# Gate tiles and dense tiles placed anew beside two recurrences, and an opening whose weights are issued ahead

## Chip, cores and metric

The program runs on one core of a Trainium2 chip. The metric is the device time of one execution in microseconds (us). TensorE (PE) is the matrix engine, PEld its weight loads, VectorE is DVE, ScalarE is ACT, GpSimd is POOL, and SyncE (SP) issues most DMAs.

## What is computed

Two layers of one trunk over 512 latent tokens (segment L) and 256 context tokens (segment C), 1024 channels wide. Each layer normalises its input, sends it through three mixers (RWKV-7, gated DeltaNet, attention), scales each branch by a gate computed from the same normalised input, and ends in a SwiGLU. In short:

```python
hx = modulate(rmsnorm(x, norm1[l]), sh1x, sc1x)
px = jnp.split(hx @ lp['w_in'], IN_SPLIT_POINTS, axis=-1)
ya_x, _ = rwkv_branch(hx, px[0], lp, st_a)
yb_x, _ = gdn_branch(hx, px[1], px[2], lp, st_b)
yc_x = attn_latent(px[3], px[4], kc, vc, lp, cos, sin)
gates = jax.nn.sigmoid(h @ lp['w_gate'] + lp['b_gate'])      # 3 x 1024 outputs
ga, gb, gc = jnp.split(gates, N_BRANCH, axis=-1)
m = ga * (ya @ lp['w_up_a']) + gb * (yb @ lp['w_up_b']) + gc * (yc @ lp['w_up_c'])
x = x + g1x * (m @ lp['w_out'])
x = x + g2x * swiglu(...)
```

The shifts, scales and gains (sh1x, sc1x and so on) are 6 x 1024 numbers per layer and token kind, made from the conditioning vectors by `ada_w`. In layer 0 both segments go through all of it; in the last layer the context is needed only for the states, keys and values.

## The kernel before

Channels lie on the 128 partitions, tokens along the free axis. A **dense tile** is one 128-column block of a weight matrix times the whole input: eight blocks of 128 channels, each as three fp32r products (`mm3`, lines 241 to 243: high part times high part, high times low, low times high). A tile with both segments is 24 matmuls of 512 columns (PSUM tile dL) and 24 of 256 (dC); a tile of L alone is the first 24. For each the weights are loaded by SP into `wst` (two buffers), cast by ACT to `whi` (line 227) and their rest taken by POOL as `wlo` (line 231). The 24 tiles of `w_gate` of a layer (`gate`, whose tanh on ACT is line 710) are needed only at the layer's end; their place is free.

A layer runs in this order: low-rank projections and DeltaNet's scalars (`lora_g`, `gdn_scalars`), attention, DeltaNet in two passes `p` of two heads, RWKV in four passes `j` of two heads, then the merge and the SwiGLU.

Both recurrences run over **groups** of four chunks. A pass has three: ("C", 0) the context, ("L", 0) and ("L", 1) the halves of the latent tokens. In a group some preparation (exponentials, small products, the inverse of a triangular matrix in `inverse`) precedes four **steps**, each of which needs the state that the step before left. A step's solve is line 1378 in DeltaNet and line 1074 in RWKV; stretches of a pass are given below from one solve to another. The dense tiles that fill the time beside a pass are a list `self.units`: in DeltaNet the six q, k, v tiles of the next pass (`g_tiles`), two z tiles and some gate tiles; in RWKV three r, k, v tiles of the next pass, its key norm (`r_knorm`) and some gate tiles. After a group is written, `fill(n)` writes the next n units. The tables `GD` and `RD` hold n, by pass and, in a pass, for the three groups. `flush` writes what is left, except two units in a DeltaNet pass, which stand one by one behind the two heads' output norms.

Instructions aren't run in the order written: a scheduler orders them on each engine from priorities and modelled costs, and the recurrences' groups are written under a raised priority (`HPG`, `HPR`), so that a unit written behind a group lands among its steps or among those of the groups before it.

The **opening** (`build`) loads the context, then four 512 KB tiles for the first ada block (`ada`: products of the conditioning vectors with a block of `ada_w` in `adaps`, a copy to `adasb`, and a transposing product in `adamp`), the latent tokens, the weights of the first low-rank projection, and three more ada blocks, with eight buffers for their tiles. Then `norm1` makes the normalised input `hh`, `hl`. The second low-rank projection's weights (256 to 383 of `l1`) are loaded and split inside `lora_g` in layer 0; in layer 1 they have been made ahead, as `self.second`.

Of the kernel before, what the change touches and what calls it, by code (L numbers as in the profile page):

```python
# [38 lines left out]
AD = (0, 1, 2, 3)  # L39
ORD = (1, 2, 3, 6, 5, 7, 4)  # L40
LOV = ((1,), (1, 3, 5))
GD = ((5, 4, 0), (5, 4, 0))
RD = ((4, 4, 0), (4, 4, 0), (4, 4, 0), (2, 2, 0))


PV = {}
# [157 lines left out]
class Prog:  # L204
# [75 lines left out]
    def build(self):  # L280
        nc, tc, A = self.nc, self.tc, self.A
        self.pend = {"L": [], "C": []}
        pool = lambda name, bufs=1, **k: tc.tile_pool(name=name, bufs=bufs, **k)
        with tc.block(name="whole", schedule_with_timeline_sim=True), pool("cst") as cst, pool("wp", 2) as wp, pool("pp", 2, space=bass.MemoryType.PSUM) as pp, \
                pool("dr", space=bass.MemoryType.DRAM) as dr, pool("hp") as hp, pool("sb", 2) as sb:
            self.cst, self.wp, self.pp, self.dr, self.hp, self.sb = cst, wp, pp, dr, hp, sb
            self.dC, self.dc = pp.tile([128, 2, TC], F32, name="dC", tag="dC", bufs=1), 0
            C = cst.tile([128, NCO], F32, name="C")
            nc.sync.dma_start(C, A["co"][:, 0:NCO])
            self.C = C  # L290
            self.scv = cst.tile([128, 8, 32], F32, name="scv")
            nc.sync.dma_start(self.scv, A["cv"])
            nc.scalar.activation(self.scv, self.scv, AF.Silu)
            self.xsrc = {"C": A["xT"][:, :, 0:TC], "L": A["xT"][:, :, TC:T]}
            self.vectors(0)
            with tc.tile_pool(name="nx", bufs=2, reuse_waits="tile") as nx:
                x = {}
                self.nb = 8
                self.segs = ["L", "C"]
                ss = self.sums()  # L300
                self.tables()
                for s, n in (("C", TC), ("L", TL)):
                    x[s] = nx.tile([128, KT, n], F32, name="x" + s, bufs=1)
                    nc.sync.dma_start(x[s], self.xsrc[s])
                    if s == "C":
                        self.ada(0, 0, nx, 8, bank=("dL", 2))
                    else:
                        self.first = self.split(self.lora(0, 384, 96, 2, nx)[:])
                    for k in range(KT):
                        self.squares(x[s][:, k, :], k, s, ss)  # L310
                    self.settle()
                    rs = sb.tile([128, TL + 4], F32, name="rs", tag="up", bufs=2)[:, :n]
                    self.rstd_from(rs, ss[s], 1.0 / D, self.co("cb", 0, 1))
                    for k in range(KT):
                        nc.vector.tensor_tensor(x[s][:, k, :], x[s][:, k, :], rs, ALU.mult)
                for i in range(1, 4):
                    self.ada(0, i, nx, 8, bank=("dL", 2))
                self.norm1(0, x, nx)
            for l in range(DEPTH):
                self.l, self.nb = l, SB[l]  # L320
                self.last = l == DEPTH - 1
                self.P, self.MOD = self.Ps[l], self.MODs[l]
                self.layer()
                if self.upto is not None and self.upto[0] == l:
                    break
# [9 lines left out]
        self.nc.sync.dma_start(self.Ps[l], self.A["pv"][l])  # L335
        self.MODs[l] = self.cst.tile([128, 48, 2], F32, name=f"MOD{l}")

    def ada(self, l, n, pool, bufs=4, share=False, tag="adaw", bank=("iv", 1)):

        nc, A = self.nc, self.A  # L340
        ps = self.pp.tile([128, 512], F32, name="adaps", tag=bank[0], bufs=bank[1])
# [7 lines left out]
                nc.tensor.matmul(ps[32 * g:32 * g + 32, :], self.scv[:, k, :], w[:, i, :], start=(k < 4), stop=(k >= 4))  # L349
        sb = pool.tile([128, 512], F32, name="adasb", tag="adasb", bufs=1)  # L350
        nc.scalar.copy(sb, ps)
        mp = self.pp.tile([128, 4, 2], F32, name="adamp", tag=bank[0], bufs=bank[1])
        for m in range(4):
            nc.tensor.matmul(mp[:, m, :], sb[:, 128 * m:128 * m + 128], self.co("sel2"), start=True, stop=True)
        ob, _ = PV["ada_b"]
# [237 lines left out]
    def layer(self):  # L593
# [14 lines left out]
        with pool("sx") as self.sx:  # L608
# [10 lines left out]
            with pool("sg") as self.sc:  # L619
# [4 lines left out]
                    u()  # L624
                for p in range(2):
                    self.units = (g_tiles(1) if p == 0 else []) + z_tiles(p)
                    if p == 1:
                        self.units += gates[:6]
                        del gates[:6]
                    self.settle()  # L630
                    self.g_begin(p)
                    for grp, n in zip((("C", 0), ("L", 0), ("L", 1)), GD[p]):
                        with tc.high_priority(offset=HPG[l]):
                            self.g_group(p, *grp)
                        self.fill(min(n, len(self.units) - 2))
                    self.flush(2)
                    for hh in range(2):
                        self.g_out(p, hh)
                        self.fill(1)
# [3 lines left out]
        with pool("sr") as self.sc:  # L643
# [16 lines left out]
            self.settle()  # L660
            for j in range(4):
                self.units = r_tiles(j + 1) if j < 3 else []
                take = len(gates) if j == 3 else 4
                self.units += gates[:take]
                del gates[:take]
                self.r_begin(j)
# [90 lines left out]
    def lora_g(self):  # L757

        nc, A, l, sc = self.nc, self.A, self.l, self.sc
        self.GC, self.BR, self.rw, self.re, gh = {}, {}, {}, {}, {}  # L760
        if l:
            wq, wm = self.second
        else:
            wq, wm = self.lora(l, 256, 128, 2, sc)
            wm = self.split(wm[:])
        ps = self.dense(*self.first, self.h, self.S12)
        for s in self.S12:
            n = TL if s == "L" else TC
# [965 lines left out]
```

## Time and profile before

| what | value |
|---|---|
| median of 3 runs | 3975.29 us (3964.88 to 3981.9) |
| the profiled execution | 3986.69 us, of which the span of its instructions is 3984.9 us |
| TensorE busy | 3572.3 us, 90% of the span |
| VectorE, ScalarE, GpSimd busy | 2426.7, 1681.5 and 1465.1 us |
| mean granted TensorE clock | 0.906 |
| read from and written to HBM | 257.87 and 34.23 MB |

The profile page counts an engine as busy while an instruction of it executes. PEclk is the share of full speed that TensorE's clock was granted: 1.00 is 2.4 GHz, 0.50 is 1.2 GHz. A row of the windows view gives a stretch's start and end in us from the span's start, its length, then for each engine the busy us and in brackets the instructions, then the mean granted clock, the share of the DMA engines' time, and GB/s. A row of the timeline gives start, length, engine, line, operation, tiles, shapes, and in square brackets how long the engine had been idle and what ended that.

### The profile page before, as it was taken

The numbers are of one execution on the slowest core, as the hardware profiler recorded it, in microseconds if no ns is written. First come the engines' busy times: TensorE is split into PE (matmuls) and PEld (weight loads), VectorE is DVE, ScalarE is ACT, GpSimd is POOL, SyncE is SP. The second block draws the span as 40 slices with busy tenths as digits, with TensorE's granted clock in tenths as the row PEclk, the third lists the DMA queues.
The fourth block names the chain that finished last, engine by engine and source line by source line (L and its number), as shares of the span: only waits on it lengthen the run. The fifth ranks groups of instructions, "written<-read, shape, count | busy, mean of one in ns | idle before, by whom it ended". The sixth has DMA issues, their size and how long they took to land. (4 is left out here: it accounts for less than half of the span.)

```text
span 3984.9 us, 69791 instructions
## 1 busy us (share of the span) xinstructions
PE 3572.3 (90%) x27704; PEld 2928.8 (73%) x27704; DVE 2426.7 (61%) x4776; ACT 1681.5 (42%) x3207; POOL 1465.1 (37%) x1738
## 2 busy tenths in 40 slices
PE   7987878999899989899999798889998999898998
PEld 4655667777777768789999656666777777677887
DVE  5386745326766746565555557965167786467776
ACT  5455534334444432333333646543343443234334
POOL 3223213244233315454444424414241333164554
PEclk7998878999799999999999899989796988699999
DMA  5501111111011126422222251102120111252232
GB/s 190 172 30 51 32 33 50 53 57 55 13 53 38 40 71 199 153 80 69 70 69 59 94 179 53 51 25 75 39 63 9 53 32 47 96 186 66 93 96 82
DMA packets 121174, 296.61 MB, mean 74 GB/s; under 512 B 15024, under 2 KB 41824, under 8 KB 120464
## 3 DMA queue, kind: packets, MB, share of 16 engines
q1 hardware_dynamic: 111408, 260.16, 20.9%
q0 software_dynamic: 9440, 31.99, 2.1%
q8 instruction: 218, 3.57, 0.4%
q14 instruction: 108, 0.88, 0.1%
HBM read 257.87 MB, written 34.23 MB: 73 GB/s over the span
## 5 line engine op out<-in xcount | busy, mean ns | idle before, releaser
L231 POOL TENSOR_TENSOR wlo<-wst,whi 128x512 fp32r<-128x512 f32 (+3 forms) x606 | 693.0, 1164 | 784.1 <-ACT whi L227 755.4
L227 ACT CAST whi<-wst 128x1024 fp32r<-128x1024 f32 (+3 forms) x303 | 266.0, 878 | 512.3 <-PE dC L243 193.4
L241 PE MATMUL dL<-hh,whi 128*128 128x512 f32 x1040 | 436.3, 420 | 21.3 <-ACT tg L710 4.5
L242 PE MATMUL dL<-hl,whi 128*128 128x512 f32 x1040 | 423.7, 407 | 3.7 <-DVE hl L407 2.3
L243 PE MATMUL dL<-hh,wlo 128*128 128x512 f32 x1040 | 422.8, 407 | 0.1
L241 PEld LDWEIGHTS dL<-hh,whi 128*128 128x128 f32 x1040 | 202.1, 194 | 79.6 <-issue 6.9
L242 PEld LDWEIGHTS dL<-hl,whi 128*128 128x128 f32 x1040 | 201.9, 194 | 51.5 <-issue 7.5
L241 PE MATMUL dC<-hh,whi 128*128 128x256 f32 x704 | 220.7, 313 | 18.4 <-ACT ct L371 9.3
L243 PEld LDWEIGHTS dL<-hh,wlo 128*128 128x128 f32 x1040 | 201.3, 194 | 48.3 <-issue 2.5
L242 PE MATMUL dC<-hl,whi 128*128 128x256 f32 x704 | 213.2, 303 | 4.8 <-DVE hl L407 2.4
L243 PE MATMUL dC<-hh,wlo 128*128 128x256 f32 x704 | 212.2, 301 | 0.0
L502 POOL TENSOR_TENSOR sl<-S,sh 128x512 fp32r<-128x512 f32 x110 | 152.7, 1392 | 154.8 <-ACT sh L501 115.4
L241 PE MATMUL q<-g2h,sh 128*128 128x384 f32 (+1 forms) x528 | 166.8, 318 | 16.3 <-DVE c L524 13.8
L241 PEld LDWEIGHTS dC<-hh,whi 128*128 128x128 f32 x704 | 144.9, 206 | 35.3 <-ACT ct L371 11.9
L242 PE MATMUL q<-g2l,sh 128*128 128x384 f32 (+1 forms) x528 | 166.6, 316 | 2.9 <-DVE g2l L447 2.9
L243 PE MATMUL q<-g2h,sl 128*128 128x384 f32 (+1 forms) x528 | 165.1, 314 | 0.0
L242 PEld LDWEIGHTS dC<-hl,whi 128*128 128x128 f32 x704 | 145.2, 206 | 13.0 <-issue 3.9
L501 ACT CAST sh<-S 128x512 fp32r<-128x512 f32 x176 | 105.0, 619 | 105.0 <-PE q L242 63.7
L243 PEld LDWEIGHTS dC<-hh,wlo 128*128 128x128 f32 x704 | 145.1, 206 | 3.2 <-issue 1.7
L524 DVE TENSOR_TENSOR c<-c,q 128x384 f32<-128x384 f32 (+1 forms) x220 | 106.0, 482 | 61.7 <-PE q L243 50.6
L241 PE MATMUL dL<-fh,whi 128*128 128x512 f32 x352 | 138.3, 393 | 3.0 <-ACT fh L578 1.6
L242 PE MATMUL dL<-fl,whi 128*128 128x512 f32 x352 | 138.1, 392 | 0.0
(545 smaller groups left out, 10008.8 us busy)
## 6 DMA issues: line engine op xcount, KB each, us to landing
adaw<-in_ada SPq DMA_DIRECT2D x96, 512.0 KB
wst<-in_win SPq DMA_DIRECT2D x68, 512.0 KB
wst<-in_wg SPq DMA_DIRECT2D x48, 512.0 KB
w<-in_f SPq DMA_DIRECT2D x45, 512.0 KB
wst<-in_f SPq DMA_DIRECT2D x43, 512.0 KB
t<-tg POOLq DMA_DIRECT2D x48, 256.0 KB, 2.6
tgL<-t SPq DMA_DIRECT2D x48, 256.0 KB
wst<-in_f SPq DMA_DIRECT2D x48, 256.0 KB
```

The lines of the kernel that those rows point to most:

```text
L227: nc.scalar.copy(hi, wt)
L231: nc.gpsimd.tensor_tensor(lo[:, a:b], wt[:, a:b], hi[:, a:b].bitcast(F32), ALU.subtract)
L241: nc.tensor.matmul(ps, wh, xh, start=first, stop=False)
L242: nc.tensor.matmul(ps, wh, xl, start=False, stop=False)
L243: nc.tensor.matmul(ps, wl, xh, start=False, stop=last)
L501: nc.scalar.copy(hi, src)
L502: (nc.vector if i in LOV[l] else nc.gpsimd).tensor_tensor(lo, src, hi[:].bitcast(F32), ALU.subtract)
L524: add = lambda d, a, b: nc.vector.tensor_tensor(d, a, b, ALU.add)
```

## The change

Four edits. The tables: of a layer's 24 gate tiles, four stand in DeltaNet's first pass and eight in its second (before, none and six); RWKV's first three passes have two each (before, four), its last the six that are left, as before. The numbers behind the groups are (4, 4, 2) in DeltaNet's first pass, (3, 3, 2) in its second, (2, 2, 2) in RWKV's first three and, as before, (2, 2, 0) in its last. In the opening, ada blocks 1 to 3 are written ahead of the first low-rank projection's weights, with 12 buffers in place of 8, and `adamp` takes another PSUM tag (`ch`) than `adaps`. And the second low-rank projection's weights are loaded and split ahead of `norm1`, in layer 0 as in layer 1. The matmuls are the same in number and shape.

```diff
-GD = ((5, 4, 0), (5, 4, 0))
-RD = ((4, 4, 0), (4, 4, 0), (4, 4, 0), (2, 2, 0))
+GD = ((4, 4, 2), (3, 3, 2))
+RD = ((2, 2, 2), (2, 2, 2), (2, 2, 2), (2, 2, 0))
...
-                        self.ada(0, 0, nx, 8, bank=("dL", 2))
+                        self.ada(0, 0, nx, 12, bank=("dL", 2), mbank=("ch", 2))
                     else:
+
+                        for i in range(1, 4):
+                            self.ada(0, i, nx, 12, bank=("dL", 2), mbank=("ch", 2))
                         self.first = self.split(self.lora(0, 384, 96, 2, nx)[:])
...
-                for i in range(1, 4):
-                    self.ada(0, i, nx, 8, bank=("dL", 2))
+                wq, wm = self.lora(0, 256, 128, 2)
+                self.second = wq, self.split(wm[:])
                 self.norm1(0, x, nx)
...
-        mp = self.pp.tile([128, 4, 2], F32, name="adamp", tag=bank[0], bufs=bank[1])
+        mbank = mbank or bank
+        mp = self.pp.tile([128, 4, 2], F32, name="adamp", tag=mbank[0], bufs=mbank[1])
...
-                    if p == 1:
-                        self.units += gates[:6]
-                        del gates[:6]
+                    take = 8 if p else 4
+                    self.units += gates[:take]
+                    del gates[:take]
...
-                take = len(gates) if j == 3 else 4
+                take = len(gates) if j == 3 else 2
...
-        if l:
-            wq, wm = self.second
-        else:
-            wq, wm = self.lora(l, 256, 128, 2, sc)
-            wm = self.split(wm[:])
+        wq, wm = self.second
```

Three places show how the change moves instructions. First SP, the DMA queue of the opening: `adaw` are the ada blocks' tiles, `xL` the latent tokens, `l1w` the low-rank weights (96 and 128 columns wide), `wst` the first dense weights. Before:

```order
L345 DMA adaw<-in_ada 128x1024 x4
L304 DMA xL<-in_xT 128x8x512
L729 DMA l1w<-in_l 128x8x96
L345 DMA adaw<-in_ada 128x1024 x4
L236 DMA wst<-in_win 128x1024 x2
L335 DMA P_15142<-in_pv 128x233
L345 DMA adaw<-in_ada 128x1024 x8
L729 DMA l1w<-in_l 128x8x128
```

And in the changed kernel:

```order
L348 DMA adaw<-in_ada 128x1024 x4
L304 DMA xL<-in_xT 128x8x512
L348 DMA adaw<-in_ada 128x1024 x8
L733 DMA l1w<-in_l 128x8x96
L733 DMA l1w<-in_l 128x8x128
L338 DMA P_15142<-in_pv 128x233
L348 DMA adaw<-in_ada 128x1024 x4
L236 DMA wst<-in_win 128x1024
```

Two ada blocks now follow the latent tokens at once, both low-rank loads stand ahead of the last block, and the dense weights behind it.

Second ACT, in DeltaNet's first pass of layer 0, between the second and the third solve of group ("L", 0): `GUs` is the copy of a solve, `GS` the state, `go` the output, W and Y belong to the next group's inverse. Before:

```order
L1380 COPY GUs<-GU 128x256
L917 ACTIVATE W<-X,C 128x16x16
L1405 COPY go<-GSO 128x2x64
L1369 ACTIVATE GS<-GS,egl 128x128 x2
L917 ACTIVATE W<-X,C 128x16x16
L1405 COPY go<-GSO 128x2x64
L1369 ACTIVATE GS<-GS,egl 128x128 x2
L941 COPY Y<-ips 128x512
L1380 COPY GUs<-GU 128x256
```

One step of the same group in the changed kernel:

```order
L1380 COPY GUs<-GU 128x256
L917 ACTIVATE W<-X,C 128x16x16
L1405 COPY go<-GSO 128x2x64
L1369 ACTIVATE GS<-GS,egl 128x128 x2
L1405 COPY go<-GSO 128x2x64
L1369 ACTIVATE GS<-GS,egl 128x128 x2
L941 COPY Y<-ips 128x512
L714 ACTIVATE tg<-dL,hb 128x512
L227 CAST whi<-wst 128x1024
L1380 COPY GUs<-GU 128x256
```

A gate tile's tanh and the next tile's cast have come in between two solves that had no dense tile between them.

Third ACT, in RWKV's first pass of layer 0, around the third and fourth solve: `UV` is the copy of a solve, S the state, `tg` the tanh of a gate tile. Before:

```order
L951 COPY TT<-ips 32x8x32
L227 CAST whi<-wst 128x1024
L710 ACTIVATE tg<-dC,hb 128x256
L1075 COPY UV<-Up 64x2x64
L710 ACTIVATE tg<-dL,hb 128x512
L1067 ACTIVATE S<-S,EL 128x64 x2
L227 CAST whi<-wst 128x1024
L710 ACTIVATE tg<-dC,hb 128x256
L1075 COPY UV<-Up 64x2x64
```

And in the changed kernel:

```order
L951 COPY TT<-ips 32x8x32
L1075 COPY UV<-Up 64x2x64
L1067 ACTIVATE S<-S,EL 128x64 x2
L1075 COPY UV<-Up 64x2x64
```

The gate tiles that stood among these steps are gone, and no other dense tile has taken their place.

## Rows read from the trace of the kernel before

**Rows 1.** The page: busy time by engine, and the clock in 40 slices.

```profile
PE 3572.3 (90%) x27704; PEld 2928.8 (73%) x27704; DVE 2426.7 (61%) x4776; ACT 1681.5 (42%) x3207; POOL 1465.1 (37%) x1738
...
PEclk7998878999799999999999899989796988699999
```

**Rows 2.** The chain that ended last: two dense matmuls (start, us, what).

```profile
3937.44 0.12 PE dC L241
...
3955.03 0.23 PE dL L241
```

**Rows 3.** Windows: layer 0's DeltaNet stage.

```profile
335.00:813.00 478.00, 394.62 (x3231) 320.69 (x3230) 265.99 (x536) 210.15 (x398) 131.24 (x204) 0.84 0.16 47
```

**Rows 4.** Timeline of PE in the opening.

```profile
40.90 3.21 PE L349 MATMUL adaps<-adaw,scv 128*32 128x512 f32 x16
44.88 1.05 PE L354 MATMUL adamp<-C,adasb 128*128 128x2 f32 x8 [0.77 <-ACT adasb L351]
47.03 0.58 PE L241 MATMUL dC<-hh,whi 128*128 128x256 f32 x1 [1.10 <-ACT hh L405]
...
64.55 0.39 PE L243 MATMUL dL<-hh,wlo 128*128 128x512 f32 x1
68.63 0.39 PE L1205 MATMUL tsp<-C,gcC 40*64 40x8 f32 x4 [3.70 <-DVE gcC L1176]
...
93.22 0.73 PE L241 MATMUL dL<-ghgL,g2h 128*128 128x512 f32 x2
```

**Rows 5.** Timeline of SP: the load of the second low-rank weights.

```profile
50.45 0.55 SPq L729 DMA_DIRECT2D l1w<-in_l  x1
```

**Rows 6.** A window of the opening, for the last two columns (DMA share, GB/s).

```profile
20.00:30.00 10.00, 5.23 (x14) 0.89 (x14) 7.69 (x11) 5.22 (x9) 2.93 (x2) 0.67 1.03 405
```

**Rows 7.** Windows in DeltaNet, three of layer 0, then two of layer 1.

```profile
543.40:597.80 54.40, 38.86 (x368) 32.72 (x369) 23.82 (x58) 12.85 (x39) 8.76 (x14) 0.61 0.11 32
712.90:769.70 56.80, 54.02 (x502) 44.96 (x502) 26.83 (x54) 17.28 (x44) 20.26 (x23) 0.97 0.18 57
769.70:786.00 16.30, 11.61 (x120) 9.21 (x120) 5.19 (x19) 3.68 (x11) 0.00 (x0) 0.95 0.01 2
2576.10:2615.60 39.50, 35.03 (x322) 26.17 (x321) 31.47 (x51) 26.76 (x47) 13.33 (x19) 0.91 0.14 41
2615.60:2655.80 40.20, 30.80 (x424) 25.45 (x425) 23.26 (x59) 15.51 (x48) 5.78 (x10) 0.90 0.14 41
```

**Rows 8.** Windows for line 241 alone, columns PE, PEld, clock, DMA share, GB/s.

```profile
543.40:597.80 54.40, 0.00 (x0) 0.00 (x0) 0.61 0.11 32
712.90:769.70 56.80, 19.80 (x55) 10.79 (x55) 0.97 0.18 57
```

**Rows 9.** Windows of RWKV passes, three of layer 0, then three of layer 1.

```profile
945.40:1062.20 116.80, 104.89 (x1351) 87.50 (x1352) 71.60 (x186) 39.30 (x100) 29.26 (x43) 0.81 0.11 37
...
1227.80:1376.80 149.00, 137.85 (x1578) 110.67 (x1577) 95.50 (x246) 69.03 (x142) 47.98 (x69) 0.93 0.14 43
1376.80:1460.20 83.40, 74.05 (x1068) 60.62 (x1067) 45.94 (x122) 30.04 (x78) 20.85 (x24) 0.96 0.12 36
2975.20:3079.80 104.60, 92.95 (x1177) 77.57 (x1178) 75.02 (x184) 36.99 (x96) 20.41 (x35) 0.67 0.08 23
3079.80:3211.50 131.70, 123.63 (x1396) 96.76 (x1394) 95.37 (x233) 58.53 (x124) 42.41 (x65) 0.90 0.13 40
3341.40:3434.90 93.50, 83.25 (x1008) 67.58 (x1002) 60.76 (x155) 33.05 (x80) 21.02 (x26) 0.79 0.10 30
```

**Rows 10.** Windows for line 241 alone in four of these passes.

```profile
945.40:1062.20 116.80, 20.64 (x60) 11.34 (x60) 0.81 0.11 37
1376.80:1460.20 83.40, 17.86 (x51) 9.65 (x51) 0.96 0.12 36
2975.20:3079.80 104.60, 7.05 (x19) 3.68 (x19) 0.67 0.08 23
3341.40:3434.90 93.50, 13.04 (x32) 6.00 (x32) 0.79 0.10 30
```

More of the change, by code (lines that the diff above doesn't have):

```diff
@@ L336, in vectors, with ada @@
         self.MODs[l] = self.cst.tile([128, 48, 2], F32, name=f"MOD{l}")
-    def ada(self, l, n, pool, bufs=4, share=False, tag="adaw", bank=("iv", 1)):
+    def ada(self, l, n, pool, bufs=4, share=False, tag="adaw", bank=("iv", 1), mbank=None):
         nc, A = self.nc, self.A
```

## Prediction, written before the change was run

> **What bounds the kernel now.** I read the page, the chain of waits, the windows by stage and then the rows of PE. The page says that PE is busy 90% of the span [rows 1], and the chain that ended last comes out of a dense matmul at full speed, 0.23 us for 512 columns and 0.12 for 256 [rows 2]. The bound is therefore TensorE's work plus the time in which it idles or runs at the lower of its two clocks (1.2 against 2.4 GHz); the clock row of the page stands at 7 in the opening's slice, 7 in the sixth (DeltaNet, layer 0), 7 in the eleventh and 6 in two later ones (RWKV's first pass in layer 0, first and last in layer 1) [rows 1]. Layer 0's DeltaNet stage has PE busy 394.62 of 478 us at a mean clock of 0.84 [rows 3]. The change leaves every matmul as it is. It can only win or lose idle time, low-clock time, and the length of the opening, so I cost it by place.
>
> A dense tile with both segments is 24 x 0.23 + 24 x 0.12 = 8.4 us, one of L alone 24 x 0.23 = 5.5 us [rows 2]. Line 241 is one matmul in three of it, so one of them stands for 8.4 / 16 = 0.525 us of dense work in layer 0 and 5.5 / 8 = 0.69 for tiles of L alone. Length minus dense work I call the net time of a stretch: what the recurrence itself costs there. Beside each place I counted dense matmuls between solves in the two orders, and call an interval of two solves bare with fewer than five (a pass has eleven).
>
> **The opening.** Before, the ada blocks end at 44.88 + 1.05 us and the first dense matmul on the input starts at 47.03 [rows 4]; the queue runs at 405 GB/s with the DMA engines always busy [rows 6]. After, two ada blocks follow the latent tokens at once, and ahead of the last block the two dense weights (1 MB) are replaced by the second low-rank load (0.5 MB): 0.5 MB is 1.3 us at 405 GB/s. The remaining blocks can then follow each other, limited by a block's own 3.21 us of products and some 2 us of transposing [rows 4]. I take 5 us off the start of the input (3 to 5). Larger is the second projection. Its weights are issued at 50.45 [rows 5]; PE is done with the first projection at 64.9, at 0.39 us per 512-column matmul, which is the low clock, idles 3.70 us for VectorE's scan, and reaches the products with `g2h` only at 93.22 [rows 4]. In the new order the second projection's matmuls are interleaved with the first's, into the time in which the input is still being made. They are 24 x 0.39 = 9.4 us for L and about half, 4.7, for C. I take the L part as gone from the path: 5 + 9 = **14 us** (3, the input alone, to 5 + 14 = 19). The two VectorE products and the cast for these weights move ahead of `norm1`, into engines that wait for the loads there, and I cost them at nothing; without that cover they would be some 2 us. The loads that are passed over, the two dense weights, are wanted only behind both projections.
>
> **DeltaNet.** In layer 0's first pass the stretch over group ("L", 0) is 54.40 us, PE busy 38.86, clock 0.61 [rows 7], and not one line-241 matmul in it [rows 8]. Its counterpart in the second pass is 56.80 us at 0.97 [rows 7] with 55 of them [rows 8], that is 28.9 us of dense work and a net time of 27.9. So cover is worth up to 54.4 - 27.9 = 26.5 us there, and filling its idle alone 54.40 - 38.86 = 15.5. The new order puts the equivalent of 100 matmuls of 512 columns, 23 us, into that group, and bare intervals fall from 8 to 4: I take **24** (15 to 27). The second pass loses three bare steps of 16.30 us to one; their idle is 4.7 [rows 7], I take **4** (0 to 5). In layer 1's first pass two such stretches of 39.50 and 40.20 us have 4.5 and 9.4 us of idle at 0.91 and 0.90 [rows 7]; four tiles of L come in, but mostly beside the context group, and bare intervals fall only from 8 to 6: **9** (5 to 14). Layer 1's second pass keeps 5 bare intervals: **0** (3 faster to 5 slower). DeltaNet together 37 us (15 to 49).
>
> **RWKV.** What DeltaNet gains in cover RWKV loses, 12 gate tiles in two layers. Layer 0's first pass goes from 6 bare intervals to 8. Now it is 116.80 us [rows 9] with 60 line-241 matmuls [rows 10], net 85.3; layer 1's first pass, with 9 bare ones, is 104.60 at clock 0.67 [rows 9] with 19 [rows 10]; at 0.6 us for each, a mixture, net 93.2. The difference, **8 us**, is what I charge (0 to 15). The second and third passes go from 2 bare intervals to 6. Layer 1's second pass has 4 and runs at 0.90, layer 0's third at 0.93 [rows 9]; that drop of 0.03 on some 124 us of PE is **4 us for each** of the two (0 to 8). In layer 1 the first three passes lose tiles of L alone, 5.5 us in place of 8.4, so **3 us each** (0 to 5). The two last passes keep their tiles: 0. Together 8 + 8 + 9 = 25 us slower (0 to 46). The third numbers of 2 change little in this: the tiles written behind the second L group stand earlier in the order, and the last steps of the passes stay bare. The ACT and POOL work of a gate tile moves with it, and its loads stay as many; in the first pass, POOL was busy 29.26 of 116.80 us, ACT 39.30 [rows 9], so neither becomes the bound where the tiles leave, and in DeltaNet's stage, with 265.99, 210.15 and 131.24 of 478 us for VectorE, ACT and POOL [rows 3], there is room for four more.
>
> **Sum.** -14 - 37 + 25 = -26 us. The profiled execution, 3986.69 us, would become 3960.7; it was 11.4 us over the median of 3975.29, so on the median I forecast **3949.3**. The ends added up are -19 - 49 + 0 = -68 and -3 - 15 + 46 = +28.
>
> **Rivals.**
>
> *Dense work only fills idle time.* A dense tile in front of a solve delays the chain through the state, and only PE's idle time is won. For it: in the bare stretch the chain is what takes 54.40 us, and PE has 15.5 of idle [rows 7]. Against it: the counterpart holds 28.9 us of dense work in 56.80 [rows 7, 8]. DeltaNet would give 15 in place of 37: -14 - 15 + 25 = -4, **3971 us**, no change. The Trainium skill, page "TensorE: Matmul & The Clock Gate", section "The mechanism" of Part 3, says that matmuls start and end in program order, without reordering. By that rule a solve waits for all dense matmuls ahead of it, however long it has been ready, which is this rival's mechanism; the counterpart's row speaks for its costing little.
>
> *RWKV loses the clock* (the slower side). In RWKV a bare pass is dearer than I charge. Layer 0's last pass is 83.40 us at 0.96 [rows 9], with 51 line-241 matmuls [rows 10] net 56.6; layer 1's is 93.50 at 0.79 [rows 9], with 32 [rows 10] net 71.4 (0.69 each). If each of the six passes that lose tiles fell by that 14.8 us, RWKV would cost 89: -14 - 37 + 89 = +38, **4013 us**. It makes the kernel slower from 51 / 6 = 8.5 us a pass on. For it: layer 1's first pass, with the fewest dense matmuls, stands at 0.67 [rows 9]. Against it: passes two and three keep two gate tiles, three tiles of the next pass and its key norm, and layer 1's second pass shows 0.90 with little more [rows 9].
>
> *RWKV hardly loses anything.* The second and third passes hold the clock near 0.93, their extra bare intervals being filled by the preparation of the next group, and only the first passes pay: 8 + 3 = 11, so -14 - 37 + 11 = -40, **3935 us**. For it: the third pass of layer 0 has 137.85 us of PE in 149.00 [rows 9], so dense tiles there buy little but their own time.
>
> *The opening is hidden.* It gives its 3 to 5 us of earlier input only, since the chain from VectorE's scan goes on unchanged: 10 us less, 3959 us. This I count into the forecast's range.
>
> **How the numbers follow.** A measurement of this kernel can tell some 0.5%, 20 us, from no change: faster means under 3955, slower over 3995. Forecast 0.42, own range 3930 to 3980; of it 0.26 lies under 3955 and 0.16 within. RWKV loses nothing 0.22, faster. Only idle is filled 0.20: 0.03 faster, 0.15 the same, 0.02 slower. RWKV loses the clock 0.16: 0.03 the same, 0.13 slower. Sums: faster 0.51, same 0.34, slower 0.15. The range starts at 3915, which is the gain of 40 with 20 more from the ends of opening and DeltaNet, and goes to 3995, leaving out about 0.05 below and 0.15 above.
>
> **What would show it.** In the profile after: the first dense matmul on the input near 42 us and the `g2h` products near 79 (right), or 45 and 90 (opening hidden). Line-241 matmuls in group ("L", 0) of DeltaNet's first pass, with a clock over 0.9 and a net time under 31 us; a clock that stays near 0.6, or solves that wait 2 us and more behind dense matmuls, would show the first rival. RWKV's second and third pass at 0.90 and, in layer 0, a first pass with a net time near 93; clocks near 0.8 in all six would show the second. The forecast is wrong if the tiles moved into DeltaNet run as fast as before but RWKV's net time rises by more than 51 us in all.

## Result and profile after

The changed kernel takes **3996.20 us** (median of 20 runs) against 3975.26 us for the kernel before in the same series: a ratio of **1.0051, 95% interval 1.0036 to 1.0066**. It is some 20 us slower; 26 us faster had been forecast. The profiled execution has a span of 4003.0 us, 18.1 us longer than the one shown of before.

The page after, to be read against [rows 1]:

```profile
PE 3610.9 (90%) x27704; PEld 2971.2 (74%) x27704; DVE 2434.0 (61%) x4776; ACT 1670.9 (42%) x3201; POOL 1459.8 (36%) x1738
...
PEclk8988898999779789899999799989795987699999
```

PE carries out the same 27704 matmuls but is busy 38.6 us longer. In the clock row the opening's slice has risen from 7 to 8 and the sixth (DeltaNet, layer 0) from 7 to 9; the twelfth, fourteenth and fifteenth (RWKV, layer 0) have fallen from 9 to 7, 7 and 8.

Windows of the changed kernel, over the stretches that answer to [rows 7] and [rows 9]: group ("L", 0) of DeltaNet's first pass, then RWKV's four passes of layer 0, then those of layer 1.

```profile
546.90:597.80 50.90, 47.60 (x499) 40.14 (x500) 26.16 (x57) 16.68 (x45) 16.35 (x23) 0.98 0.24 77
...
947.60:1060.30 112.70, 98.57 (x1269) 81.40 (x1268) 80.67 (x201) 35.40 (x96) 23.99 (x44) 0.70 0.07 21
1060.30:1207.20 146.90, 135.62 (x1485) 110.52 (x1485) 99.14 (x249) 61.04 (x132) 41.47 (x69) 0.80 0.09 28
1207.20:1353.90 146.70, 134.85 (x1485) 109.63 (x1484) 101.01 (x249) 60.53 (x130) 40.06 (x59) 0.80 0.09 28
1353.90:1450.20 96.30, 88.95 (x1147) 72.94 (x1146) 58.15 (x155) 39.18 (x93) 24.16 (x31) 0.96 0.11 36
2998.90:3101.80 102.90, 85.57 (x1112) 73.03 (x1113) 67.59 (x177) 30.89 (x86) 12.00 (x27) 0.55 0.03 8
3101.80:3228.50 126.70, 113.33 (x1348) 90.50 (x1344) 93.79 (x233) 55.71 (x120) 35.72 (x59) 0.87 0.10 30
3228.50:3356.80 128.30, 112.75 (x1328) 90.16 (x1326) 92.18 (x227) 54.66 (x118) 34.44 (x55) 0.83 0.09 29
3356.80:3450.90 94.10, 87.38 (x1002) 70.48 (x998) 59.24 (x155) 32.99 (x80) 21.88 (x26) 0.74 0.09 30
```

The bare DeltaNet group is cured: clock 0.98 where it was 0.61. In RWKV the second and third passes of layer 0 stand at 0.80; they were at 0.94 and 0.93. The first passes fell from 0.81 to 0.70 and from 0.67 to 0.55.

Two passes of before that [rows 9] does not show, RWKV's second of layer 0 and its third of layer 1:

```profile
1062.20:1227.80 165.60, 153.26 (x1692) 122.79 (x1686) 116.51 (x294) 70.09 (x149) 53.31 (x89) 0.94 0.12 36
3211.50:3341.40 129.90, 121.58 (x1374) 94.25 (x1372) 94.43 (x227) 57.39 (x122) 41.87 (x61) 0.88 0.14 41
```

A pass is compared by its net time, as in the prediction: its length less the dense work in it, one line-241 matmul standing for 0.525 us in layer 0 and, as a mixture, for 0.6 us in layer 1. Those are counted that begin in the stretch. Line 241 alone, the kernel before in RWKV's second pass and the changed one in the first three passes of layer 0 (of the 25 in the first row, one began before the pass):

```profile
1062.20:1227.80 165.60, 46.05 (x126) 24.75 (x126) 0.94 0.12 36
```

```profile
947.60:1060.30 112.70, 7.88 (x25) 4.53 (x24) 0.70 0.07 21
1060.30:1207.20 146.90, 29.09 (x80) 15.13 (x80) 0.80 0.09 28
1207.20:1353.90 146.70, 28.45 (x80) 15.09 (x80) 0.80 0.09 28
```

The second pass is shorter, 146.9 us for 165.6, and yet dearer: 165.6 - 126 x 0.525 = 99.5 us net before, 146.9 - 80 x 0.525 = 104.9 after. Summed in this way from the two traces:

| net us, from the first solve of a pass to that of the next (the last pass: to its own last solve) | before | after | change | forecast |
|---|---|---|---|---|
| DeltaNet, layer 0, two passes | 215.7 | 180.0 | -36 | -28 |
| RWKV, layer 0, four passes | 332.1 | 372.4 | +40 | +16 |
| DeltaNet, layer 1 | 195.5 | 197.0 | +2 | -9 |
| RWKV, layer 1 | 347.5 | 369.9 | +22 | +9 |

DeltaNet's two passes of layer 1, before and after, hold 27 and 72, then 67 and 80 line-241 matmuls:

```profile
2576.10:2702.10 126.00, 101.89 (x1110) 80.92 (x1109) 80.09 (x171) 54.02 (x123) 30.55 (x45) 0.81 0.13 39
2702.10:2831.00 128.90, 117.30 (x980) 92.18 (x979) 57.84 (x134) 45.27 (x98) 37.72 (x44) 0.84 0.17 51
```

```profile
2567.60:2724.20 156.60, 131.75 (x1238) 103.69 (x1237) 92.86 (x194) 65.53 (x137) 52.27 (x68) 0.85 0.19 55
2724.20:2852.80 128.60, 120.78 (x993) 97.09 (x992) 49.75 (x111) 42.89 (x97) 34.59 (x38) 0.85 0.20 59
```

The price of a tile matters in layer 1: at 0.69 us, that of tiles of L alone, DeltaNet comes out 3 us faster and RWKV 27 slower. The first solve of DeltaNet comes 7.4 us earlier (486.3 to 478.9 us); the stretch from DeltaNet to RWKV in layer 0 wins 7 us net, for which nothing was forecast, and in layer 1 it loses 1; the two tails lose 4 together. -7 - 36 + 40 + 2 + 22 - 7 + 1 + 4 = +19, for a difference of the spans of 18.

PE's idle time, length less busy time, tells the two layers apart. Over RWKV's four passes of layer 0 it is 44.8 us before and 44.6 after, so the 40 us lie in matmuls that take longer, while the mean granted clock falls from 0.91 to 0.81. In layer 1 the idle time rises from 38.3 to 53.0 us: some 15 us of that loss are idle. Single passes are less sure than these sums, since small matmuls also move over their borders: the second pass of layer 0 has 66 fewer than before, the last 44 more.

### The profile page after: what moved, and what is told of

It is laid out like the page before. It is cut to its first block, busy times and chain, and to the rows that moved or that the text cites. A ratio compares the mean times of both kernels' runs of the same rounds, so it can differ in the third digit from the quotient of the medians.

```text
span 4003.0 us, 69824 instructions
## 1 busy us (share of the span) xinstructions
PE 3610.9 (90%) x27704; PEld 2971.2 (74%) x27704; DVE 2434.0 (61%) x4776; ACT 1670.9 (42%) x3201; POOL 1459.8 (36%) x1738
## 5 line engine op out<-in xcount | busy, mean ns | idle before, releaser
L241 PE MATMUL dL<-hh,whi 128*128 128x512 f32 x1040 | 435.0, 419 | 18.1 <-ACT up L724 4.6
L716 POOL DMA_DIRECT2D t<-tg x72 | 40.4, 562 | 272.8 <-ACT tg L714 260.7
```

Of the source, the lines that this page charges most:

```text
L241: nc.tensor.matmul(ps, wh, xh, start=first, stop=False)
L716: nc.gpsimd.dma_start(self.td[:, m, t0:t0 + n], t)
```

## Experiments

The theory at the start: the change wins in the opening and in layer 0's DeltaNet, and loses more in RWKV, whose last groups run at the lower clock since their tiles went. The rivals: the opening costs; the table that spreads tiles over three groups costs; the middle passes of layer 0 alone cost. Each ratio is to the kernel before, run beside it.

**The opening alone.** The change's opening, with old counts and tables:

```diff
-GD = ((4, 4, 2), (3, 3, 2))
-RD = ((2, 2, 2), (2, 2, 2), (2, 2, 2), (2, 2, 0))
+GD = ((5, 4, 0), (5, 4, 0))
+RD = ((4, 4, 0), (4, 4, 0), (4, 4, 0), (2, 2, 0))
...
-                    take = 8 if p else 4
-                    self.units += gates[:take]
-                    del gates[:take]
+                    if p == 1:
+                        self.units += gates[:6]
+                        del gates[:6]
...
-                take = len(gates) if j == 3 else 2
+                take = len(gates) if j == 3 else 4
```

> The kernel before with the change's opening alone (12 buffers, ada blocks 1 to 3 ahead, the second low-rank weights ahead of the input); gates and tables as before. Theory (the change loses in RWKV and wins in the opening and in DeltaNet): 7 us faster than before, ratio 0.998, since the first solve of DeltaNet came 7.4 us earlier with the whole change. Rival A (the opening is what costs, its earlier start being paid back in attention and DeltaNet): 0 to 20 us slower. The prediction's own term was 14 us faster, 0.9965.

Measured 1.0026 (1.0012 to 1.0039), 10 us slower. The first solve of DeltaNet comes 6.4 us earlier, at 479.9 us, as foreseen, yet RWKV of layer 0 is longer, net 343.4 us for 332.1. Neither the theory nor the prediction had that. Rival A has the number right but not the place, since DeltaNet of layer 0 pays nothing back (net 214.3 us for 215.7).

**Counts and tables alone**, on the old opening:

```diff
-GD = ((5, 4, 0), (5, 4, 0))
-RD = ((4, 4, 0), (4, 4, 0), (4, 4, 0), (2, 2, 0))
+GD = ((4, 4, 2), (3, 3, 2))
+RD = ((2, 2, 2), (2, 2, 2), (2, 2, 2), (2, 2, 0))
...
-                    if p == 1:
-                        self.units += gates[:6]
-                        del gates[:6]
+                    take = 8 if p else 4
+                    self.units += gates[:take]
+                    del gates[:take]
...
-                take = len(gates) if j == 3 else 4
+                take = len(gates) if j == 3 else 2
```

> The kernel before with the change's gate counts and tables alone; the opening as before. Theory: the 12 gate tiles taken from RWKV cost more than DeltaNet wins with them: 28 us slower than before, ratio 1.007, with DeltaNet's four passes some 45 us better in idle time plus half of the low-clock time, RWKV's eight some 80 us worse, its last groups in layer 0's second and third passes at a clock near 0.5. Rival A (the opening costs): within 5 us of before, ratio 1.000.

Measured 1.0081 (1.0062 to 1.0100), 30 us slower, where 28 were expected: DeltaNet of layer 0 net 181.8, RWKV of layer 0 378.2, of layer 1 357.8. The tables carry the loss. Its parts are smaller than expected: RWKV's eight passes are 56 us worse, not some 80.

**Layer 0 alone**, with the new opening:

```diff
+GO = ((5, 4, 0), (5, 4, 0))
+RO = ((4, 4, 0), (4, 4, 0), (4, 4, 0), (2, 2, 0))
...
-                    take = 8 if p else 4
+                    take = (6 * p) if l else (8 if p else 4)
...
-                take = len(gates) if j == 3 else 2
+                take = len(gates) if j == 3 else (4 if l else 2)
```

with `GO` and `RO` read in layer 1.

> The changed kernel with layer 1's gates and tables as before, so that only layer 0 moves six gate tiles. Theory: in layer 0 gain and loss nearly cancel (45 us against 47), in layer 1 the tiles of L bring DeltaNet nothing (they land beside the context group, which is covered) and cost RWKV 35 us with 6 us back; without that the kernel is 27 us faster than the changed one, ratio to before 0.998. Rival B (it is layer 0's second and third RWKV passes alone, where the clock fell to 0.5, that cost): near the changed kernel, ratio 1.003 or more.

Measured 1.0002 (0.9986 to 1.0018). Beside this opening layer 1's part of the change costs some 20 us, where 27 were expected, and rival B is out.

**The old table for RWKV**, counts as changed:

```diff
-RD = ((2, 2, 2), (2, 2, 2), (2, 2, 2), (2, 2, 0))
+RD = ((4, 4, 0), (4, 4, 0), (4, 4, 0), (2, 2, 0))
```

> The changed kernel with RWKV's table alone back at (4, 4, 0), gate counts as changed. Theory (the number of tiles decides, and the tiles written behind the last group run earlier anyhow, so no last group has a dense tile with either table): within 4 us of the changed kernel, ratio to before 1.005. Rival C (the spread over three groups is what costs): 15 us or more faster than the changed kernel, ratio under 1.001.

Measured 1.0081 (1.0060 to 1.0101). The old table doesn't give the loss back; if anything it is 12 us slower than the changed kernel, more than the 4 us allowed. The spread is not what costs.

**The kernel before once more**, for its stage lengths.

> The kernel before once more, for a second profile of it. If stage lengths are a property of the order, the stages agree with the first profile within 2 us each but for single groups whose clock fell differently; the first profiled execution was 11 us above the median, and the theory is that those 11 us lie in one or two recurrence passes with a lower granted clock. Rival: they are spread evenly.

3980.07 us. RWKV's first pass of layer 0 in the second profile, and then two passes of layer 1 (to be held against [rows 9]: 116.80, 104.60 and 131.70 us):

```profile
942.80:1060.30 117.50, 104.88 (x1353) 87.11 (x1354) 71.49 (x186) 39.40 (x100) 29.23 (x42) 0.81 0.12 36
...
2974.60:3079.10 104.50, 92.86 (x1175) 77.51 (x1176) 74.93 (x184) 36.96 (x96) 20.37 (x35) 0.67 0.08 23
3079.10:3210.90 131.80, 123.71 (x1400) 96.85 (x1396) 95.22 (x233) 58.55 (x124) 43.06 (x65) 0.90 0.14 40
```

Passes agree within about 1.3 us but for the last one of layer 1, which was 93.5 us and is 89.3, at 0.87 for 0.79; the stretch from DeltaNet to RWKV in layer 0 was 159.4 us and is 154.9, and DeltaNet's first solve came at 486.3 and comes at 488.8. So stage lengths go with the order, and single places move by 2 to 5 us. Of the 7 us that the changed kernel wins in that stretch, 4.5 are within what two profiles of before differ by.

**The second low-rank weights alone**:

```diff
+                wq, wm = self.lora(0, 256, 128, 2)
+                self.second = wq, self.split(wm[:])
                 self.norm1(0, x, nx)
...
-        if l:
-            wq, wm = self.second
-        else:
-            wq, wm = self.lora(l, 256, 128, 2, sc)
-            wm = self.split(wm[:])
+        wq, wm = self.second
```

> The kernel before with the second low-rank weights loaded and split ahead of the input, and nothing else of the change. Theory F (the opening's gain is real but small, and is lost in layer 0's recurrences, whose order the scheduler makes anew whenever anything ahead of them moves): products with g2h 9 us earlier or more, first solve of DeltaNet 3 to 6 us earlier, the whole between 5 us faster and 10 us slower, with RWKV of layer 0 taking what is lost. Rival G (the reordered ada blocks and the 12 buffers are what costs in the opening kernel): 5 us or more faster than before.

Measured 1.0022 (1.0008 to 1.0037). The first solve of DeltaNet is at 481.4 us, 5 to 7 earlier than in the two profiles of before; RWKV of layer 0 is net 342.0. Theory F holds so far, and rival G is out.

**Twelve buffers alone**, which add no instruction:

```diff
-                        self.ada(0, 0, nx, 8, bank=("dL", 2))
+                        self.ada(0, 0, nx, 12, bank=("dL", 2))
...
-                    self.ada(0, i, nx, 8, bank=("dL", 2))
+                    self.ada(0, i, nx, 12, bank=("dL", 2))
```

> The kernel before with 12 buffers in place of 8 for the opening's ada tiles and nothing else: no instruction is added or taken out, but the scheduler's order of the recurrences comes out as in the opening kernel (the same dense matmuls between solves in layer 0's RWKV passes). Theory F (the opening kernels lose what they win because the order of the recurrences is made anew): the loads land a little earlier or not, and the whole is 3 to 12 us slower than before, ratio 1.001 to 1.003, with RWKV of layer 0 longer by some 8 us. Rival G (the opening's own edits cost): within 2 us of before.

Measured 1.0029 (1.0016 to 1.0042), 11 us slower. RWKV's four passes of layer 0 in this kernel:

```profile
942.50:1064.30 121.80, 106.71 (x1361) 88.73 (x1362) 80.33 (x197) 43.09 (x110) 32.67 (x48) 0.81 0.12 35
1064.30:1218.60 154.30, 142.97 (x1626) 114.78 (x1622) 108.55 (x268) 65.69 (x139) 51.58 (x84) 0.92 0.13 39
1218.60:1380.50 161.90, 149.71 (x1640) 120.22 (x1639) 110.39 (x272) 71.91 (x151) 49.61 (x74) 0.92 0.13 40
1380.50:1467.80 87.30, 78.14 (x1066) 64.57 (x1065) 46.12 (x122) 30.44 (x78) 20.84 (x24) 0.89 0.11 35
```

With 59, 115, 122 and 51 line-241 matmuls they are net 343.1 us, where the second profile of before has 333.9: nine of the eleven us. The order of PE's matmuls in the trace differs from before's in the recurrences of both layers, by some 4400 lines of a comparison, with the same 27704 matmuls, and DeltaNet's first solve comes at 485.9 us, where the two profiles of before have 486.3 and 488.8. So what the opening kernels lose goes with the order that the scheduler makes anew behind such an edit, without the change's new order of the opening's loads. Why this order is dearer was not separated, nor whether four more buffers, which can also move tiles in memory, cost in another way.

**Tiles held in the bare groups.** If place is what counts, tiles forced into the last groups should win. A tile written behind a latent group is issued on PE in portions, each behind a solve of that group:

```diff
+        span, self.span = getattr(self, "span", None), None
...
-                self.mm3(ps, wh[:, k, :], wl[:, k, :], xh[:, off + k, :], xl[:, off + k, :],
-                         first=(k == 0), last=(k == kt - 1))
+                q = list(segs).index(s) * kt + k
+                hold = self.tc.issue_after(self.steps[span[q * len(span) // (kt * len(segs))]]) if span else nullcontext()
+                with hold:
+                    self.mm3(ps, wh[:, k, :], wl[:, k, :], xh[:, off + k, :], xl[:, off + k, :],
+                             first=(k == 0), last=(k == kt - 1))
...
-        for u in self.units[:n]:
+        for i, u in enumerate(self.units[:n]):
+            self.span = behind[i] if i < len(behind) else None
             u()
```

`steps` collects the solves of the pass, and `behind` names steps of the group. First with nearly the old counts, two tiles to a latent group (one in the last group of RWKV's last pass), and tables to match:

> The kernel before with its gate counts nearly kept (0 and 6 in DeltaNet, 4, 4, 3 and 7 in RWKV), but each tile written behind a latent group is held on TensorE behind that group's own solves, in portions of eight to sixteen matmuls, so that the last groups get two tiles each. Theory P (what counts is where a tile lands: in a bare group it gives back idle time and half of the low-clock time, beside a covered one nothing): bare intervals fall from 66 to 25, the last groups of the passes run above a clock of 0.9 in place of 0.5 to 0.9, 60 to 120 us faster than before, ratio 0.970 to 0.985. Rival D (dense matmuls ahead of a solve delay the chain as much as they fill): within 20 us of before or slower, the clock high but the net time of the groups unchanged.

Then with the changed kernel's counts and opening, where RWKV's first three passes have one tile to a latent group:

> The changed kernel, its gate counts (4 and 8 in DeltaNet, 2, 2, 2 and 6 in RWKV) and its opening kept, with the tiles behind latent groups held behind those groups' solves in the same way. Theory P: the count hardly matters once tiles lie in bare groups; 70 to 130 us faster than the changed kernel, ratio to before 0.975 to 0.990, and within 25 us of the held kernel with the old counts. Rival N (the number of tiles taken from RWKV is what cost): near the changed kernel, 1.000 or more.

Measured 1.0077 (1.0049 to 1.0105) and 1.0077 (1.0055 to 1.0100): some 30 us slower each, where 60 to 130 faster was expected. The three groups of RWKV's first pass of layer 0, in the kernel before (second profile), all and line 241 alone:

```profile
942.80:986.70 43.90, 42.81 (x514) 35.29 (x513) 18.40 (x48) 13.82 (x32) 15.57 (x19) 0.96 0.22 67
986.70:1035.80 49.10, 41.79 (x494) 34.57 (x493) 36.23 (x97) 17.50 (x47) 11.62 (x16) 0.76 0.08 26
1035.80:1057.90 22.10, 18.24 (x311) 15.61 (x310) 16.27 (x41) 7.82 (x20) 2.04 (x7) 0.61 0.01 2
...
942.80:986.70 43.90, 17.08 (x48) 9.36 (x48) 0.96 0.22 67
986.70:1035.80 49.10, 4.11 (x12) 2.27 (x12) 0.76 0.08 26
```

and in the held kernel with the old counts:

```profile
924.50:962.50 38.00, 33.34 (x398) 27.51 (x398) 18.69 (x47) 12.96 (x34) 4.77 (x9) 0.60 0.02 7
962.50:1008.50 46.00, 41.93 (x511) 34.94 (x508) 28.61 (x72) 18.47 (x46) 12.51 (x19) 0.93 0.12 40
1008.50:1045.20 36.70, 36.41 (x442) 29.43 (x440) 25.70 (x69) 14.07 (x32) 9.48 (x15) 1.00 0.10 33
...
924.50:962.50 38.00, 3.85 (x8) 1.89 (x8) 0.60 0.02 7
962.50:1008.50 46.00, 12.05 (x32) 6.84 (x32) 0.93 0.12 40
1008.50:1045.20 36.70, 11.40 (x32) 6.04 (x32) 1.00 0.10 33
```

The clock does what theory P said: the last two groups rise from 0.76 and 0.61 to 0.93 and 1.00. But the context group lost its tiles and fell from 0.96 to 0.60. Net, the groups are 18.7, 42.8 and 22.1 us before, and 33.8, 29.2 and 19.9 held: 83.6 against 82.9, no gain at all. Over layer 0's RWKV the held kernel is net 353.1 us for 333.9, with more idle time in the third pass (18.0 us for 11.1). Theory P falls; of rival D the clock and the missing gain agree. How much of the loss is dense matmuls standing ahead of solves, and how much the groups that they left, the runs don't separate.

The sum hides a difference between the recurrences. Over both layers, at the prices above, DeltaNet's passes are 34 us better in the held kernel with the old counts than in the second profile of before, and RWKV's are 38 us worse. In the held kernel with the new counts RWKV of layer 0 has a clock of 0.83, 0.86, 0.84 and 0.89 in its four passes, where the changed kernel has 0.70, 0.80, 0.80 and 0.96; yet it is net 376.8 us for 372.4. Its busy time beyond the dense work is 15 us less, and its idle time 20 us more (64.4 us for 44.6): what the clock gave back there, idle time took.

**Layer 0 alone on the old opening**, the change's counts and tables there:

> The kernel before with layer 0's gate counts and tables of the change, layer 1 and the opening as before. From the stages of the tables kernel: DeltaNet of layer 0 some 30 us better in idle time plus half of the low-clock time, RWKV of layer 0 some 54 us worse, so 20 to 28 us slower than before, ratio 1.005 to 1.007. Rival (the layer 0 move pays, as the layer 0 kernel with the new opening, 1.0002 against 1.0026 for the opening alone, suggests): 5 to 12 us faster, 0.997 to 0.999.

Measured 1.0054 (1.0035 to 1.0073), as expected. RWKV of layer 0 is net 372.2, DeltaNet 181.1; the profiled execution is the fastest of six, 16 us under their median, so its stages don't show the whole loss. The rival's observation stands all the same: beside the new opening the same move makes the kernel some 8 us faster (3989.10 us with the opening alone, 3981.45 with layer 0's move added), beside the old one 20 slower. Layer 1's part, too, costs 20 us beside the new opening and 11 beside the old (1.0081 against 1.0054). The parts of the change don't add up, and no run shows why.

**Four tiles, then three, to the first DeltaNet pass only**; layer 0's counts are 4 and 6 in DeltaNet with 2, 4, 4 in RWKV, then 3 and 6 with 3, 4, 4 (what is left goes to the last pass, four tiles), layer 1 and the opening as before:

```diff
-GD = ((5, 4, 0), (5, 4, 0))
+GD = (((4, 4, 2), (5, 4, 0)), ((5, 4, 0), (5, 4, 0)))
+TG = ((3, 6), (0, 6))
+TR = ((3, 4, 4), (4, 4, 4))
...
+                    take = TG[l][p]
...
-                take = len(gates) if j == 3 else 4
+                take = len(gates) if j == 3 else TR[l][j]
```

> The kernel before with four gate tiles beside DeltaNet's first pass in layer 0 alone, two of them taken from RWKV's first pass and two from its last; the second pass keeps six, the middle passes of RWKV four, layer 1 is as before. Theory (a tile is worth what its group lacks): the bare group of DeltaNet's first pass wins about 29 us, RWKV's first pass loses 13, its last some 12, and the order of the rest comes out as in the opening kernel, another 8: within 6 us of before. Rival (cover is worth the same wherever it lies): 10 us or more slower.

> As the kernel before this one, but three tiles beside DeltaNet's first pass, one from RWKV's first pass and two from its last; here the dense tiles of RWKV's second pass lie as in the kernel before (133, 107 and 12 matmuls of 512 columns in its three groups). Theory: DeltaNet's first pass wins 20 us, RWKV's first loses 3, its last 12: 5 us faster than before, ratio 0.9985. Rival as above: 10 us slower.

Measured 0.9985 (0.9969 to 1.0002) and **0.9969 (0.9951 to 0.9987)**: the second, 3970.82 us, is faster than both kernels of the study, by 8 us in the medians (12 by the ratio) against before. Its bare group of DeltaNet's first pass, and its last RWKV pass of layer 0:

```profile
549.80:598.10 48.30, 42.38 (x459) 36.37 (x458) 25.62 (x55) 14.67 (x43) 13.71 (x21) 0.93 0.21 64
...
1380.80:1450.20 69.40, 56.74 (x967) 45.81 (x966) 44.97 (x122) 25.01 (x71) 14.24 (x16) 0.95 0.07 21
```

Line 241 alone in that last pass:

```profile
1380.80:1450.20 69.40, 6.72 (x19) 3.59 (x19) 0.95 0.07 21
```

DeltaNet's first pass wins 19 us net against the second profile of before (120.7 for 139.8), where 20 were expected. The last RWKV pass gives up 32 of 51 line-241 matmuls, two tiles, and stays at 0.95: net 59.4 us for 56.5. In the kernel with four tiles it is 62.5, and the first RWKV pass, which gave up two tiles, pays 14.7 (100.7 for 86.0). So a tile's cover was cheap to take in the last pass and dear in the first. The gain of the three-tile kernel came out near its forecast partly by luck. Its first RWKV pass, charged 3 us for one tile, pays 9.2 (95.2 for 86.0), the two middle passes, which keep their tiles, pay 3 each, and the last pays 3 in place of 12. RWKV of layer 0 is then 18.5 us worse, DeltaNet of layer 0 23 better (191.7 for 215.1), and some of the 8 us lies outside both: DeltaNet begins 4.8 us earlier (484.0 for 488.8), with the opening unedited. Against the four-tile kernel, the kernel with layer 0's whole move loses 27 us by the two medians; what differs is that it takes two tiles each from the middle passes, and leaves them with DeltaNet's second pass and RWKV's last (and the numbers in the tables). How much of the 27 us each of these costs was not separated.

## Why the prediction was wrong

- **The failing step is the RWKV term**, 25 us with an upper end of 46. By the traces it is 40 + 22 = 62, more than twice what was charged. The second and third passes of layer 0 were charged 4 us each, from a drop of 0.03 in the clock; their clocks fell by 0.14 and 0.13, and their net time rose by 5.5 and 14.0 us. The counterpart was ill chosen. Layer 1's second pass has 4 bare intervals, not far from the 6 that were counted after the change; but half of its dense matmuls lie in the first latent group, and the changed passes have theirs in the context group. Line 241 alone in the context group and the first latent group, layer 1's second pass before:

```profile
3079.80:3138.50 58.70, 14.87 (x35) 7.00 (x35) 0.97 0.12 40
3138.50:3179.40 40.90, 13.91 (x37) 6.96 (x37) 1.00 0.25 72
```

  and the second pass of layer 0 after:

```profile
1060.30:1126.10 65.80, 23.71 (x65) 12.31 (x65) 1.00 0.14 44
1126.10:1166.60 40.50, 5.39 (x15) 2.83 (x15) 0.74 0.11 31
```

  Windows of the last two groups of RWKV's second pass of layer 0, before (the two rows below the dots are line 241 alone):

```profile
1128.50:1176.90 48.40, 48.40 (x557) 39.48 (x556) 31.12 (x69) 18.96 (x48) 17.18 (x23) 1.00 0.19 59
1176.90:1201.80 24.90, 17.71 (x215) 14.36 (x213) 21.20 (x63) 10.31 (x25) 7.25 (x11) 0.84 0.07 22
...
1128.50:1176.90 48.40, 16.79 (x48) 9.06 (x48) 1.00 0.19 59
1176.90:1201.80 24.90, 1.98 (x7) 1.34 (x7) 0.84 0.07 22
```

  and after:

```profile
1126.10:1166.60 40.50, 34.47 (x448) 29.23 (x447) 27.47 (x63) 14.63 (x41) 10.59 (x15) 0.74 0.11 31
1166.60:1198.40 31.80, 28.03 (x318) 23.35 (x316) 25.26 (x68) 9.60 (x24) 4.21 (x9) 0.53 0.01 1
```

  The last group loses its 7 line-241 matmuls and takes 7 us longer, at 0.53; the one before it falls from 48 to 15, and from 1.00 to 0.74: net 32.6 us for 23.2. The context group wins some of this back. In DeltaNet the prediction had priced a covered group against a bare one (26.5 us); in RWKV it took the mean clock of a whole pass instead, which does not see in which group the cover lies. In layer 1 the three passes that lose tiles were charged 3 us each for tiles of L alone, and lost 9.1, 4.6 and 8.0. The last passes, put at 0 because they keep their tiles, lost 6.1 and 0.6; layer 0's now holds 44 more small matmuls.
- **Not all of the 40 us in layer 0 need be the tiles'.** With the opening alone, and no tile moved, RWKV of layer 0 rose by 11 us; with the tables alone it rose by 46. The two don't add up to 40, so the share of each is not shown.
- **The rival that came true**, by its sign and nearly by its number, is the loss of the clock. Its deciding point was 8.5 us a pass, 51 in all, and RWKV rose by 62; the six passes that lose tiles lost 14.8, 5.5, 14.0, 9.1, 4.6 and 8.0 us (first, second and third pass of each layer), 9.3 on average, not its 14.8, at clocks of 0.55 to 0.87. In layer 0 the unchanged idle time says that the lower clock is what the passes paid; in layer 1 some 15 of the 22 us are idle time, which the clock alone does not explain. It had a chance of 0.16, and the range ended at 3995.
- **DeltaNet in layer 0 was right**, and even larger: 24 and 4 forecast, 25.5 and 10.2 found. Its bare group has 43 line-241 matmuls, net 50.9 - 43 x 0.525 = 28.3 us, under the 31 that was to show the step right. Line 241 alone:

```profile
546.90:597.80 50.90, 15.17 (x43) 8.11 (x43) 0.98 0.24 77
```

- **DeltaNet in layer 1 won next to nothing**: 9 us faster forecast, 2 slower found (3 faster at the other price). The second pass, for which nothing was forecast, is 5 us better, and the first 7 worse. The tiles landed beside the context group, as the prediction itself saw, and at the end of the first pass a new wait came in. Timeline of PE there:

```profile
2708.88 0.40 PE L242 MATMUL dL<-hl,whi 128*128 128x512 f32 x1
2719.13 1.12 PE L1353 MATMUL gtp<-C,kc 128*128 128x128 f32 x4 [9.86 <-DVE gb L1342]
```

  A dense tile is begun and left for 9.86 us, while PE waits for VectorE's `gb` of the next pass, and VectorE in turn for its loads, which SP issued at 2700.13 and 2702.32 us, and for GpSimd. With the tables alone the same wait is 8.76 us. No run separated what made the loads late.
- **The opening was right in place and half in size.** The input starts 4.0 us earlier (5 forecast). The products with `g2h` start 11.1 us earlier, and 7.4 us are left at DeltaNet's first solve (9.9 against the second profile of before), for 14. Timeline of PE after, beside [rows 4]:

```profile
43.05 0.58 PE L241 MATMUL dC<-hh,whi 128*128 128x256 f32 x1 [1.10 <-ACT hh L409]
...
69.78 0.50 PE L241 MATMUL dL<-hh,whi 128*128 128x512 f32 x1 [1.97 <-ACT up L724]
...
82.07 0.73 PE L241 MATMUL dL<-ghgL,g2h 128*128 128x512 f32 x2 [0.86 <-ACT ghgL L789]
```

  One reading in it was false: a matmul of 0.39 us isn't one at the low clock. Between 56 and 66 us of the kernel before, at a clock of 0.94, these matmuls start 0.23 us apart:

```profile
60.03 0.39 PE L243 MATMUL dL<-hh,wlo 128*128 128x512 f32 x1
60.26 0.40 PE L241 MATMUL dL<-hh,whi 128*128 128x512 f32 x1
```

  The 0.39 is the time from start to end of one in a pipelined row; 24 of them take 5.5 us, not 9.4. And the other loss was in no step: an edit of the opening makes the order behind it anew, and with the buffers alone such a new order cost 11 us.
- **Dense work only fills idle time**, the rival with 3971 us, isn't what the bare DeltaNet group shows: it won 26 us net (54.4 to 28.3), above the 15.5 of its idle time. The Trainium skill, page "TensorE: Matmul & The Clock Gate", Part 3, section "The mechanism", says that matmuls start and end in program order. By that rule a solve waits for the dense matmuls that stand ahead of it. In this group the wait left a gain above the idle time, so it cost little. The held kernels, where dense matmuls stand among the steps on purpose, are where it may cost: DeltaNet wins there and RWKV loses, and the runs don't show that cost apart.

## What to carry to other kernels

When cover moves from one place to another, price the place that loses it in the same way as the place that gains it, group by group and by the dense matmuls in the group, not by the mean clock of a whole pass. Take it from where a row shows that the clock holds without it; here that was RWKV's last pass, where two tiles cost 3 us, while one from the first pass cost 9. Where a scheduler makes the order, an edit that should cost nothing, such as four more buffers, moved this kernel by 0.3%, so an expected gain below that is settled only by a run.

## What was not expected of the hardware

Lengths of passes are very reproducible where the order is the same. RWKV's second pass of layer 1 took 131.7 or 131.8 us in both profiles of before, in the kernel with four tiles and in that with three, at 0.90 each time, though it began up to 13 us apart; PE's order through layer 1's recurrences is nearly the same in all four. The clock of this stretch went with the work, not with the time. It isn't always so: in the last pass of layer 1, with the same order, the granted clock was 0.79 in one profile of before and 0.87 in the other three, which was worth 4 us.
